# Large fp32r matmuls that read and write their columns as two halves in turn

## The chip, the cores and the metric

The kernel runs on one core of one Trainium2 chip. The metric is the device time of one execution in microseconds (us). One execution was profiled; its trace is what the prediction reads.

## What is computed

A trunk of two layers on x (1, 256, 2048) in float32. Each layer has a token mixer and a gated ConvFFN, and each of these is followed by `x <- LayerNorm(ALPHA * x + sublayer(x))`. Cut to what matters:

```python
def hgrn2_mixer(x, w_in, norm_g, w_out, lb):        # layer 0, w_in: (2048, 8192)
    q, f, i, g = split(x @ w_in)                     # gated recurrence over 16 heads
    ...
    return o @ w_out                                 # (2048, 2048)

def chunked_gmlp(x, w_in, ln_g, ln_b, w_s, b_s, w_out):   # layer 1, w_in: (2048, 4096)
    u, v = split(gelu(x @ w_in))
    ...
    return (u * gate) @ w_out

def conv_ffn(x, w_up, conv_w, conv_b, w_down):       # both layers, w_up: (2048, 11264)
    a, b = split(x @ w_up)
    a = causal_depthwise_conv(a, conv_w) + conv_b    # width 3
    return (silu(a) * b) @ w_down                    # (5632, 2048)
```

Nearly all of the arithmetic is in these products of 256 tokens with large weights.

## The kernel before

**Precision.** Every large product is made of three fp32r products. A float32 operand is split into a high part (its fp32r rounding) and a low part (what is left): `X` and `Y` hold the activations transposed, as `[128 partitions, 16 blocks of k, 2 parts, 256 tokens]`, high part first. A weight chunk (`fetch`, 1 MB by a DMA of the SP queue into `raw`) is split by `convert` into `hi` (a copy on ACT, line 93) and `lo` (a subtraction on DVE, line 94), each `[128, 4, 512]`. Chunks are planned in order (`want`), fetched and converted up to three ahead (`AHEAD`), in three buffers of each kind.

**block_a** has tokens on the output's partitions. The weights are the moving operand, 512 columns of 4 bytes; 128 tokens of an activation block are the stationary one. For each k-block there are three matmuls into one PSUM bank: high activations on high weights (line 123), high on low weights (line 124), low on high weights (line 125). It is used with `X` (a quarter of HGRN's input product, half of gMLP's) and with `Y` (all products on the way out). `staggered_pass` (lines 673 to 675) is the same loop, for the last chunk of HGRN's output product.

**block_b** has features on the output's partitions. A 128 x 128 block of the weights is stationary; the activations are the moving operand. `both` (line 159) streams the high and the low part of one k-block as 512 columns against the high weights, into the two halves of a bank; `rest` (line 166) streams the 256 high columns against the low weights into the bank's second half. They alternate, and `gather` adds the two halves when the block is done. In the first block of each FFN (`halves`), `both` is issued for 128 tokens at a time: 256 columns, two runs of 128.

TensorE issues in program order; in front of each matmul stands the load of its 128 x 128 stationary operand.

**Places.** `cp` holds a pad, `X`, a pad of `PAD_Y` bytes, `Y`, `z` and a pad of `PAD1`; `wp` holds three buffers each of `raw`, `hi` and, after a gap of `PAD_LO` bytes, `lo`. By these pads, in each partition, `X` and `hi` begin on a multiple of 256 bytes, `Y` and `lo` 128 bytes past one. A k-block takes 2048 bytes in `X` and `Y` (1024 for each part) and in `hi` and `lo`.

Of the kernel before, what the change touches and what calls it, by code (L numbers as in the profile page):

```python
# [15 lines left out]
P = 128  # L16
S = 256
# [9 lines left out]
CK = 4  # L27
# [2 lines left out]
FFN_GROUPS = (3, 4, 4)  # L30
AHEAD = 3
LINE = 256
PAD_Y = 128
PAD_LO = 128
PAD1 = 224
BLOCK = {1: 32, 4: 32, 16: 64}
XSEQ = ((0, 2, 4), (2, 2, 0), (4, 4, 1), (8, 4, 1), (12, 4, 0))
TURN_ACT = 3


class Trunk:
# [4 lines left out]
    def __init__(self, ctx, tc, a):  # L46
        self.tc = tc
        self.nc = nc = tc.nc
        self.a = a
        self.ctx = ctx  # L50
        ent = ctx.enter_context
        self.cp = ent(tc.tile_pool(name="cp", bufs=1))
        self.wp = ent(tc.tile_pool(name="wp", bufs=3))
        self.acc = ent(tc.tile_pool(name="acc", bufs=6, space=PSUM))
        self.misc = ent(tc.tile_pool(name="misc", bufs=2, space=PSUM))
        cp = self.cp
        cp.tile([P, LINE - 128], mybir.dt.uint8, name="pad0")
        self.X = cp.tile([P, NK, 2, S], F32R, name="X")
        cp.tile([P, PAD_Y], mybir.dt.uint8, name="pady")
        self.Y = cp.tile([P, NK, 2, S], F32R, name="Y")  # L60
        self.z = cp.tile([P, 2, D], F32, name="z")
        cp.tile([P, PAD1], mybir.dt.uint8, name="pad1")
        self.small = ent(tc.tile_pool(name="small", bufs=2))
        self.plan = []
        self.issued = 0
        self.taken = 0
        self.ready = []
# [15 lines left out]
    def convert(self, raw, extra, pieces=2):  # L83
# [3 lines left out]
        if not extra:  # L87
            pool.tile([P, PAD_LO], mybir.dt.uint8, tag="gap", name="gap", bufs=1)
        lo = pool.tile([P, CK, NB], F32R, tag="lo", name="wlo")
# [20 lines left out]
    def block_a(self, act, ka, w, k0, nch, c0, evac, staggered=False, halves=False):  # L110

        nc = self.nc
        ps = [self.acc.tile([P, NB], F32, tag="acc", name="pa") for _ in range(2)]
        n = [0, 0]

        def part(ch, ci, t):
            hi, lo = ch
            for kk in range(CK):
                k = ka + ci * CK + kk
                xh = act[:, k, 0, t * P : (t + 1) * P]  # L120
                xl = act[:, k, 1, t * P : (t + 1) * P]
                last = n[t] == nch * CK - 1
                nc.tensor.matmul(ps[t], xh, hi[:, kk, :], start=n[t] == 0, stop=False)  # L123
                nc.tensor.matmul(ps[t], xh, lo[:, kk, :], start=False, stop=False)  # L124
                nc.tensor.matmul(ps[t], xl, hi[:, kk, :], start=False, stop=last)  # L125
                n[t] += 1

        take = lambda ci: self.chunk(w, k0 + ci * CK, c0)
        first = max(0, nch - 4) if staggered else nch
        head = []  # L130
        if halves:
            head = [take(ci) for ci in range(min(3, nch))]
            for t in range(2):
                for ci, ch in enumerate(head):
                    part(ch, ci, t)
        for ci in range(len(head), first):
            ch = take(ci)
            for t in range(2):
                part(ch, ci, t)
        held = [take(ci) for ci in range(first, nch)]  # L140
        for t in range(2):
            for i, ch in enumerate(held):
                part(ch, first + i, t)
            if held:
                evac(t, ps[t])
        if not held:
            for t in range(2):
                evac(t, ps[t])

    def block_b(self, act, w, nch, c0, evac, halves=False):  # L150


        nc = self.nc
        ps = [self.acc.tile([P, 2, S], F32, tag="acc", name="pb") for _ in range(4)]
        last = nch * CK - 1

        def both(ch, k, j, s=slice(0, S), start=True):
            c = slice(j * P, (j + 1) * P)
            nc.tensor.matmul(  # L159
                ps[j][:, :, s], ch[0][:, k % CK, c], act[:, k, :, s],  # L160
                start=start and k == 0, stop=k == last, skip_group_check=halves,
            )

        def rest(ch, k, j):
            c = slice(j * P, (j + 1) * P)
            nc.tensor.matmul(  # L166
                ps[j][:, 1, :], ch[1][:, k % CK, c], act[:, k, 0, :],
                start=False, stop=False, skip_group_check=halves,
            )

        def one(ch, k, j):
            for m in (rest, both) if k else (both, rest):
                m(ch, k, j)

        first = 0
        if halves:
            first = nch
            held = [self.chunk(w, ci * CK, c0) for ci in range(nch)]
            for t in range(2):
                for k in range(last):  # L180
                    for j in range(4):
                        both(held[k // CK], k, j, slice(t * P, (t + 1) * P), t == 0)
            for k in range(last):
                for j in range(4):
                    rest(held[k // CK], k, j)
            for j in range(4):
                one(held[-1], last, j)
        for ci in range(first, nch):
            ch = self.chunk(w, ci * CK, c0)
            ks = range(ci * CK, (ci + 1) * CK)  # L190
            if ci < nch - 1:
                order = [(k, j) for k in ks for j in range(4)]
            else:
                order = [(k, j) for j in range(4) for k in ks]
            for k, j in order:
                one(ch, k, j)
        for j in range(4):
            evac(j, ps[j])
# [100 lines left out]
    def turn(self, t, k0, n=4, g=None, b=None):  # L299
# [7 lines left out]
        if g is not None:  # L307
            src = self.lnp.tile([P, n, P], F32, tag="turn", name="turn", bufs=2)
            for j in range(n):
                gk, bk = self.c(g, k0 + j), self.c(b, k0 + j)  # L310
                if j < TURN_ACT:
                    nc.scalar.activation(src[:, j, :], ps[:, j, :], AF.Identity, bias=bk, scale=gk)
# [348 lines left out]
    def staggered_pass(self, act, ka, w, k0):  # L661

        nc = self.nc
        ev = [self.add_z(c, last=True) for c in range(4)]
        held = [self.chunk(w, k0, c * NB) for c in range(4)]
        for t in range(2):
            for c in range(4):
                hi, lo = held[c]
                ps = self.acc.tile([P, NB], F32, tag="acc", name="pa")
                for kk in range(CK):  # L670
                    xh = act[:, ka + kk, 0, t * P : (t + 1) * P]
                    xl = act[:, ka + kk, 1, t * P : (t + 1) * P]
                    nc.tensor.matmul(ps, xh, hi[:, kk, :], start=kk == 0, stop=False)  # L673
                    nc.tensor.matmul(ps, xh, lo[:, kk, :], start=False, stop=False)  # L674
                    nc.tensor.matmul(ps, xl, hi[:, kk, :], start=False, stop=kk == CK - 1)  # L675
                ev[c](t, ps)


# [219 lines left out]
```

## Time and profile before

| | before |
|---|---|
| median of 3 runs | 2282.81 us (2282.72 to 2283.09) |
| the profiled execution | 2282.26 us |
| its span | 2280.6 us |
| granted TensorE clock | 0.998 |
| instructions of TensorE | 12781 matmuls, 12781 weight loads |
| HBM | 425.98 MB read, 188 GB/s over the span |

How to read the lines that follow. PE is TensorE's matmuls, PEld its weight loads, DVE the vector engine, ACT the scalar engine, POOL GpSimd, SP the engine whose queue issues the large DMAs. A group line has the line of the kernel, the engine, the operation, output and inputs by their names, shapes and count, then busy time in us and the mean of one in ns, then the idle time ahead of them. A line of a stretch has its two ends, its length, the busy time and the number of matmuls in it, the granted clock, the share of the DMA engines and GB/s. A piece of the chain has its start and its length in us, the engine, the tile, the line and how many instructions were merged. A line of the timeline has start and length in us. A matmul's length in the trace reaches past the start of the next one, so the distance of starts, and not the length, says how fast they follow each other.

### The profile page before, as it was taken

Reading aid. Unit: us, or ns where it says so; the run is one execution under the profiler, and the core shown is the slowest. Engines: PE = TensorE matmul, PEld = TensorE weight load, DVE = VectorE, ACT = ScalarE, POOL = GpSimd, SP = SyncE. Lnnn points to the kernel's source line nnn. Section 1 sums busy time; section 2 is a strip of 40 time slices with the busy share of each in tenths; the row PEclk is TensorE's granted clock in tenths of the full one; section 3 lists DMA queues with packets and bytes.
Section 4 is the critical chain, followed back from the end, with each engine's and each line's share of the span. In section 5 each row is a group of like instructions: output and inputs, shape, how many; then the busy total and the mean of one; then the engine's idle time right before and its main releaser. Section 6 shows DMA issues by size and latency. Waiting matters only on the chain.

```text
span 2280.6 us, 31751 instructions
## 1 busy us (share of the span) xinstructions
PE 2258.8 (99%) x12781; PEld 1925.7 (84%) x12781; DVE 1473.4 (65%) x2327; ACT 1105.4 (48%) x1698; POOL 48.5 (2%) x102
## 2 busy tenths in 40 slices
PE   8999999999999999999999999999999999999998
PEld 7888888889888888888888888888888888888886
DVE  5777677667665665456666676566765666465655
ACT  5666565545443444344444545455444444344542
POOL 3000000000000000000000000000000000000000
PEclk9999999999999999999999999999999999999999
DMA  7454645645565555555555676655565555555563
GB/s 260 151 181 140 198 149 167 206 166 200 186 227 196 186 185 187 199 186 185 187 196 175 208 218 183 230 177 181 185 234 180 196 186 193 193 185 187 183 203 111
DMA packets 214052, 430.14 MB, mean 189 GB/s; under 512 B 7544, under 2 KB 8336, under 8 KB 213904
## 3 DMA queue, kind: packets, MB, share of 16 engines
q1 hardware_dynamic: 209536, 415.26, 54.5%
q0 software_dynamic: 4368, 12.85, 1.9%
q8 instruction: 100, 1.64, 0.3%
q14 instruction: 48, 0.39, 0.0%
HBM read 425.98 MB, written 2.10 MB: 188 GB/s over the span
## 4 chain that ended last, share of the span: by engine, by line
PE 97%; DVE 2%; ACT 1%; DMA 0%; issue 0%; SPq 0%; DVEq 0%; ACTq 0%
PE pb L159 38%; PE pb L166 20%; PE pa L123 12%; PE pa L125 12%; PE pa L124 12%; DVE wlo L94 1%; PE pl L550 1%; PE pt L305 1%; ACT whi L93 0%; PE pg L752 0%; PE pa L673 0%; PE pa L675 0%; PE pa L674 0%; DMA z<-in_x_dram 0%; PE po L522 0%; PE pout L642 0%
## 5 line engine op out<-in xcount | busy, mean ns | idle before, releaser
L94 DVE TENSOR_TENSOR wlo<-raw,whi 128x1024 fp32r<-128x1024 f32 (+1 forms) x786 | 930.6, 1219 | 693.3 <-ACT whi L93 684.9
L159 PE MATMUL pb<-X,whi 128*128 128x512 f32 (+1 forms) x3960 | 1335.1, 388 | 1.9 <-DVE X L317 1.9
L93 ACT CAST whi<-raw 128x1024 fp32r<-128x1024 f32 (+1 forms) x786 | 790.2, 1047 | 894.8 <-PE pb L159 418.7
L166 PE MATMUL pb<-X,wlo 128*128 128x256 f32 x3840 | 1049.7, 281 | 0.0
L159 PEld LDWEIGHTS pb<-X,whi 128*128 128x128 f32 x3960 | 725.0, 188 | 160.1 <-DVE X L317 2.3
L166 PEld LDWEIGHTS pb<-X,wlo 128*128 128x128 f32 x3840 | 715.7, 189 | 6.1
L123 PE MATMUL pa<-whi,Y 128*128 128x512 f32 x928 | 365.4, 394 | 0.0
L125 PE MATMUL pa<-whi,Y 128*128 128x512 f32 x928 | 363.5, 392 | 0.0
L124 PE MATMUL pa<-wlo,Y 128*128 128x512 f32 x928 | 361.2, 389 | 0.0
L125 PEld LDWEIGHTS pa<-whi,Y 128*128 128x128 f32 x928 | 173.9, 187 | 40.4
L124 PEld LDWEIGHTS pa<-wlo,Y 128*128 128x128 f32 x928 | 174.3, 188 | 37.8
L123 PEld LDWEIGHTS pa<-whi,Y 128*128 128x128 f32 x928 | 174.9, 188 | 35.6
L204 ACT COPY rest<-pb 128x256 f32<-128x256 f32 x240 | 87.9, 369 | 110.9 <-PE pb L159 92.9
L123 PE MATMUL pa<-whi,X 128*128 128x512 f32 x256 | 101.8, 398 | 0.0
L124 PE MATMUL pa<-wlo,X 128*128 128x512 f32 x256 | 101.4, 396 | 0.0
L125 PE MATMUL pa<-whi,X 128*128 128x512 f32 x256 | 100.6, 393 | 0.0
L803 DVE SCALAR_TENSOR_TENSOR act<-a,cols,act 128x254 f32<-128x254 f32 (+1 forms) x176 | 73.2, 481 | 0.0
L125 PEld LDWEIGHTS pa<-whi,X 128*128 128x128 f32 x256 | 48.1, 188 | 11.8
L123 PEld LDWEIGHTS pa<-whi,X 128*128 128x128 f32 x256 | 48.1, 188 | 11.4
L124 PEld LDWEIGHTS pa<-wlo,X 128*128 128x128 f32 x256 | 48.2, 188 | 10.6
L397 DVE TENSOR_TENSOR z<-z,pa 128x512 f32<-128x512 f32 x40 | 27.4, 684 | 34.5 <-PE pa L125 30.3
L807 ACT ACTIVATE act<-act 128x256 f32<-128x256 f32 x88 | 33.8, 415 | 8.7 <-DVE act L803 8.5
(164 smaller groups left out, 1033.2 us busy)
## 6 DMA issues: line engine op xcount, KB each, us to landing
raw<-in_ffn_w_up_dram SPq DMA_DIRECT2D x176, 1024.0 KB, 4.9
raw<-in_ffn_w_down_dram SPq DMA_DIRECT2D x88, 1024.0 KB, 4.9
raw<-in_hg_w_in_dram SPq DMA_DIRECT2D x63, 1024.0 KB, 5.1
raw<-in_sg_w_in_dram SPq DMA_DIRECT2D x32, 1024.0 KB, 5.5
raw<-in_hg_w_out_dram SPq DMA_DIRECT2D x16, 1024.0 KB, 4.9
raw<-in_sg_w_out_dram SPq DMA_DIRECT2D x16, 1024.0 KB, 4.9
g<-in_ln_g_dram POOLq DMA_DIRECT2D x16, 256.0 KB, 6.5
b<-in_ln_b_dram POOLq DMA_DIRECT2D x16, 256.0 KB, 8.8
```

The costliest lines, as they stand in the source:

```text
L93: nc.scalar.copy(hi[:, s, :], raw[:, s, :])
L94: self.last_lo = nc.vector.tensor_tensor(lo[:, s, :], raw[:, s, :], hi[:, s, :].bitcast(F32), ALU.subtract)
L123: nc.tensor.matmul(ps[t], xh, hi[:, kk, :], start=n[t] == 0, stop=False)
L124: nc.tensor.matmul(ps[t], xh, lo[:, kk, :], start=False, stop=False)
L125: nc.tensor.matmul(ps[t], xl, hi[:, kk, :], start=False, stop=last)
L159: nc.tensor.matmul(ps[j][:, :, s], ch[0][:, k % CK, c], act[:, k, :, s], start=start and k == 0, stop=k == last, skip_group_check=halves,)
L166: nc.tensor.matmul(ps[j][:, 1, :], ch[1][:, k % CK, c], act[:, k, 0, :], start=False, stop=False, skip_group_check=halves,)
L204: nc.scalar.copy(r, ps[:, 1, :])
L305: nc.tensor.transpose(ps[:, j, :], self.z[:, t, k * P : (k + 1) * P], self.ident)
L397: nc.vector.tensor_tensor(zz, zz, ps, ALU.add)
L803: nc.vector.scalar_tensor_tensor(cv[:, d:], x[:, : S - d], self.c(("cw", l, 2 - d), f), cv[:, d:], ALU.mult, ALU.add,)
L807: nc.scalar.activation(cv, cv, AF.Silu)
```

## The change

Every large matmul of 512 columns, and `rest` with 256, gets its moving operand and its output through a new view `lines`: the columns are cut into two halves, and runs of `RUN` = 16 columns are taken from the first and the second half in turn. Each column still goes to its own place; only the order within a matmul is another. The halved matmuls of `both` keep theirs. The pad between `X` and `Y` is dropped, so that `Y` begins on a multiple of 256 bytes, as `X` and `hi` do; `PAD1` shrinks by 128, which leaves `hi` on such a multiple; the gap ahead of `lo` becomes 64 bytes.

```diff
-PAD_Y = 128
-PAD_LO = 128
-PAD1 = 224
+RUN = 16
+PAD_LO = 64
+PAD1 = 96
...
+def lines(x):
+
+    return x.rearrange("p (h n c) -> p n h c", h=2, c=RUN)
...
         self.X = cp.tile([P, NK, 2, S], F32R, name="X")
-        cp.tile([P, PAD_Y], mybir.dt.uint8, name="pady")
         self.Y = cp.tile([P, NK, 2, S], F32R, name="Y")
...
-                nc.tensor.matmul(ps[t], xh, hi[:, kk, :], start=n[t] == 0, stop=False)
-                nc.tensor.matmul(ps[t], xh, lo[:, kk, :], start=False, stop=False)
-                nc.tensor.matmul(ps[t], xl, hi[:, kk, :], start=False, stop=last)
+                o, h, l = lines(ps[t]), lines(hi[:, kk, :]), lines(lo[:, kk, :])
+                nc.tensor.matmul(o, xh, h, start=n[t] == 0, stop=False)
+                nc.tensor.matmul(o, xh, l, start=False, stop=False)
+                nc.tensor.matmul(o, xl, h, start=False, stop=last)
...
         def both(ch, k, j, s=slice(0, S), start=True):
             c = slice(j * P, (j + 1) * P)
+            o, x = ps[j][:, :, s], act[:, k, :, s]
+            if s.stop - s.start == S:
+                o, x = (lines(y.rearrange("p i t -> p (i t)")) for y in (o, x))
             nc.tensor.matmul(
-                ps[j][:, :, s], ch[0][:, k % CK, c], act[:, k, :, s],
+                o, ch[0][:, k % CK, c], x,
...
-                ps[j][:, 1, :], ch[1][:, k % CK, c], act[:, k, 0, :],
+                lines(ps[j][:, 1, :]), ch[1][:, k % CK, c], lines(act[:, k, 0, :]),
```

`staggered_pass` has the same edit as `block_a`.

More of the change, by code (lines that the diff above doesn't have):

```diff
@@ L672, in staggered_pass @@
                     xl = act[:, ka + kk, 1, t * P : (t + 1) * P]
-                    nc.tensor.matmul(ps, xh, hi[:, kk, :], start=kk == 0, stop=False)
-                    nc.tensor.matmul(ps, xh, lo[:, kk, :], start=False, stop=False)
-                    nc.tensor.matmul(ps, xl, hi[:, kk, :], start=False, stop=kk == CK - 1)
+                    o, h, l = lines(ps), lines(hi[:, kk, :]), lines(lo[:, kk, :])
+                    nc.tensor.matmul(o, xh, h, start=kk == 0, stop=False)
+                    nc.tensor.matmul(o, xh, l, start=False, stop=False)
+                    nc.tensor.matmul(o, xl, h, start=False, stop=kk == CK - 1)
                 ev[c](t, ps)
```

## The prediction

> **What bounds the kernel now.** I read the page's parts 1, 2 and 4 first, then the groups by shape, then the waits of TensorE, then stretches and chain pieces that hold one kind of matmul only.
>
> ```profile
> span 2280.6 us, 31751 instructions
> ...
> PE 2258.8 (99%) x12781; PEld 1925.7 (84%) x12781; DVE 1473.4 (65%) x2327; ACT 1105.4 (48%) x1698; POOL 48.5 (2%) x102
> ...
> HBM read 425.98 MB, written 2.10 MB: 188 GB/s over the span
> ...
> PE 97%; DVE 2%; ACT 1%; DMA 0%; issue 0%; SPq 0%; DVEq 0%; ACTq 0%
> ...
> raw<-in_ffn_w_up_dram SPq DMA_DIRECT2D x176, 1024.0 KB, 4.9
> ```
> ```profile
> PE pt L305 <- DMA z<-in_x_dram: 8.0, 2, 4.3
> PE pb L159 <- DVE X L317: 1.9, 2, 1.1
> ```
>
> TensorE is the chain: 97% of the path is PE, and its two longest waits sum to 9.9 us of 2280.6. So only the spacing of matmuls can move the end. A matmul's busy time is no spacing, because each one's record overlaps the next; the counts come from the groups by shape, the spacings from stretches.
>
> ```profile
> L159 PE MATMUL pb<-X,whi 128*128 128x512 f32 x3720 | 1304.6, 395 | 0.0
> L166 PE MATMUL pb<-X,wlo 128*128 128x256 f32 x3840 | 1049.7, 281 | 0.0
> L123 PE MATMUL pa<-whi,Y 128*128 128x512 f32 x928 | 365.4, 394 | 0.0
> ...
> L123 PE MATMUL pa<-whi,X 128*128 128x512 f32 x256 | 101.8, 398 | 0.0
> ...
> L159 PE MATMUL pb<-X,whi 128*128 128x256 f32 x240 | 30.8, 285 | 1.9 <-DVE X L317 1.9
> ...
> L673 PE MATMUL pa<-whi,Y 128*128 128x512 f32 x32 | 12.8, 399 | 0.0
> ```
> ```profile
> 720.00:890.00 170.00, 170.00 (x973) 1.00 0.57 186
> 900.00:980.00 80.00, 80.00 (x351) 1.00 0.58 195
> 1270.00:1320.00 50.00, 50.00 (x216) 1.00 0.64 211
> ```
> ```profile
> 513.06 5.03 PE pb L159 x42
> ...
> 530.43 7.23 PE pb L166 x61
> ...
> 1543.33 6.67 PE pb L159 x56
> 1549.99 7.23 PE pb L166 x61
> ```
> ```profile
> 1321.40 0.87 PE pw L718 x8
> ```
>
> The first fence gives counts (L124 and L125 stand as often as L123, L674 and L675 as often as L673): 512-column matmuls 3720 + 3 x 928 + 3 x 256 + 3 x 32 = 7368, the 256-column L166 3840, and 240 halves of L159. The second gives time, matmuls and granted clock (1.00, full) in stretches of one kind (block_b; block_a on Y; block_a on X); one or two of each count began before the stretch, which sets the spread. Spacings: a pair of block_b (L159 of 512 columns and L166 of 256) 2 x 170.00/972 = 349.8 ns; block_a on Y 80.00/349.5 = 228.9 ns (228.6 to 229.2); block_a on X 50.00/214.5 = 233.1 ns (232.6 to 233.6). The third has 256-column matmuls by themselves: halves of L159 (5.03 + 6.67)/98 = 119.4 ns, L166 14.46/122 = 118.5 ns. The fourth has 128-column matmuls, each with its own load of 128 weights: 0.87/8 = 109 ns. Together the groups that the change touches hold 3720 x 0.3498 + 120 x 0.1185 + 2880 x 0.2289 + 768 x 0.2331 = 2154 us, 94% of the span.
>
> **What is lost in a spacing.** The fp32r matmuls read two things at once: the moving operand, and the weights of the next matmul.
>
> ```profile
> 640.27 0.39 PE L159 MATMUL pb<-X,whi 128*128 128x512 f32 x1
> 640.28 0.19 PEld L166 LDWEIGHTS pb<-X,wlo 128*128 128x128 f32 x1
> 640.50 0.28 PE L166 MATMUL pb<-X,wlo 128*128 128x256 f32 x1
> 640.51 0.19 PEld L159 LDWEIGHTS pb<-X,whi 128*128 128x128 f32 x1
> 640.62 0.40 PE L159 MATMUL pb<-X,whi 128*128 128x512 f32 x1
> ```
>
> The next load starts with the matmul. It reads 512 bytes of a partition in about 109 ns, while the moving operand passes about 256 columns, 1024 bytes: twice the pace. That this is felt shows in block_a: on X and on Y the same instructions run on the same moving operand, and only the stationary one lies elsewhere (X, like the high weights, begins on a multiple of 256 bytes; Y, like the low ones, 128 past it). X costs 4.2 ns more. So the place of the two reads against each other, modulo some power of two, has a price.
>
> **The change, part by part.**
> (1) Order of columns. No matmul, load, wait or transfer is added or removed. Each 512-column matmul reads 16 columns (64 bytes) of one half, then 16 of the other 1024 bytes on (L166: 512 bytes on), and writes in the same order. Seen modulo 256 bytes, two runs lie on one place, so the moving operand now advances at 64 bytes per 32 columns, the pace of the load. Before, it lapped the load about twice in each load; now their distance stays what it is at the start. If that distance is clear, the loss goes.
> (2) Pads. Y moves 128 bytes down (a multiple of 256 again), the low weights stand 64 instead of 128 past the high ones. The distances are then 0 (activations against high weights) and 64 either way (against low ones). By itself a pad costs no instruction.
> (3) Evacuation reads the same PSUM places after the last matmul: nothing moves. The 240 halved matmuls (L159 with a slice) keep their order.
>
> What a spacing is without loss has no row, so I bound it. Upper end: a 512-column matmul less a 256-column one of the same line is 256 columns streamed while hardly any load is left: (349.8 - 118.5) - 119.4 = 111.9 ns. Lower end: the 109 ns of one load, below which an L166 cannot go, taken for each 256 columns. Since a load's record lasts 0.19 us and so reaches into the second half, 111.9 still holds some loss; I take the middle, 110.5 ns per 256 columns, 221 per 512.
> - block_b pairs: 349.8 - 331.5 = 18.3 ns x 3720 = 68.1 us
> - L166 alone: (118.5 - 110.5) x 120 = 1.0 us
> - Y: (228.9 - 221) x 2880 = 22.8 us (staggered_pass's 96 within)
> - X: (233.1 - 221) x 768 = 9.3 us
>
> Sum 101.2 us. With 111.9 it is 52.5 + 0.8 + 14.7 + 7.1 = 75; with 109 it is 84.8 + 1.1 + 31.4 + 11.6 = 129. Below zero the sum can go too: see the rivals. The profiled execution took 2282.26 us (span 2280.6), 0.55 below the median of 2282.81, so no correction: 2282.3 - 101.2 = 2181 us; 2207 and 2153 are the ends.
> The Trainium skill, "TensorE: Matmul & The Clock Gate", section "Back-to-back issue gap", gives N/2.4 + 2.5 ns, 215.8 and 109.2: as an estimate by that, the sum is 144 us and the time 2138.
>
> **What is late next.** A chunk of weights feeds 16 pairs, 5.6 us now, 5.3 then. Its transfer lands in 4.9 us with three chunks in flight, and the mean rate goes from 188 to 197 GB/s, under the 211 that a stretch above already moves. Its conversion is cover enough too:
>
> ```profile
> L94 DVE TENSOR_TENSOR wlo<-raw,whi 128x1024 fp32r<-128x1024 f32 (+1 forms) x786 | 930.6, 1219 | 693.3 <-ACT whi L93 684.9
> ...
> L93 ACT CAST whi<-raw 128x1024 fp32r<-128x1024 f32 (+1 forms) x786 | 790.2, 1047 | 894.8 <-PE pb L159 418.7
> ```
>
> 2 x 1.05 us on ACT, then 2 x 1.22 on DVE per chunk; DVE's share goes from 65% to 68%. So nothing of the gain should come back as a wait.
>
> **The rivals.**
> *Jumps cost* (the other side). A matmul of 512 columns now has 32 runs, 31 jumps on both the read and the write side; L166 has 15: 7368 x 31 + 3840 x 15 = 286,008 jumps. The only jump now in the trace is the one in each half of L159 (two runs of 128 columns): 119.4 against 118.5 ns for the L166 that has none, 0.9 ns if all of it is the jump's. Then the loss is 257 us against 101 won: 2282.3 + 156 = 2438 us. It decides from 101.2 us/286,008 = 0.35 ns a jump upward. Against it: L166 loads other weights than L159 does, so the 0.9 is no clean price, and may be zero. The Trainium skill, "PSUM — Partial Sum Buffer", section "Specifications (TRN2)", speaks for this rival: its lines of PSUM are 8 bytes and any access that isn't contiguous is said to slow matmuls much. No row here shows that for runs of 64 bytes.
> *Meeting throughout.* With equal pace a bad starting distance lasts for the whole load. Now a lap spends roughly half its way near the load (64 bytes each way of 256); a meeting that never ends would double the loss: +101, 2383 us. Were it only the distance 0 (3840 L166, 2432 of block_a), their loss (52 us) and the other matmuls' gain (49) would about cancel: 2285. For it: the loads start with the matmul in the rows above, and distance 0 stands for more than half of the matmuls. Against it: the loss on X's distance 0 differs from Y's 128 by only 4.2 ns.
> *No effect.* The loss belongs to each matmul and not to meetings: 2282 us. The Trainium skill, the TensorE page again, section "Step-by-step: what each phase is for", says that the two reads have ports of their own and a load takes nothing from the running matmul. The 4.2 ns between X and Y, in the stretches above, disagree.
>
> **How the numbers follow.** Forecast 0.68; no effect 0.10; jumps cost 0.12; meeting throughout 0.10. A measurement tells 0.2%, 4.6 us, from no change. Faster: 0.68 and 0.02 of no effect (pads alone) = 0.70. Same: 0.07 of it and 0.01 of jumps near 0.35 ns = 0.08. Slower: 0.01 + 0.11 + 0.10 = 0.22. The forecast's own range is 2138 (all loss gone, and more than the rows promise) to 2265 (a sixth of the gain). To hold 8 in 10 it takes in no effect and the jumps up to about 0.5 ns, (0.5 - 0.35) x 286,008 = 42 us above 2282: 2138 to 2325, which leaves out 0.09 of meeting throughout, 0.07 of jumps and 0.03 below.
>
> **What will show it.** In block_b's stretches a pair at about 331 ns (now 349.8); block_a at about 221 on both X and Y, so that their difference is gone: that is the step of the equal pace. The 128-column and halved matmuls stay at 109 and 119.4. If the 512-column matmuls lengthen and L166 by half as much, jumps cost; if only matmuls at one distance lengthen (L123 against L124), it is the meeting. TensorE's waits should stay near 10 us. The forecast is wrong if a jump costs a third of a nanosecond, or if the starting distance of the two reads, which no row shows, is a bad one.

## The result: slower, and the profile after

The changed kernel takes 2355.65 us (median of 4 runs, 2355.60 to 2355.93) against 2282.85 beside it: a ratio of 1.0319, 95% interval 1.0301 to 1.0337. The forecast was 2181, the range 2138 to 2325; it is 73 us slower, on the other side and out of the range.

The page of the changed kernel, and the longest waits of its TensorE:

```profile
span 2353.9 us, 31751 instructions
...
PE 2333.6 (99%) x12781; PEld 1948.8 (83%) x12781; DVE 1474.2 (63%) x2327; ACT 1104.7 (47%) x1698; POOL 48.3 (2%) x102
...
PE 98%; DVE 1%; DMA 0%; issue 0%; ACT 0%; SPq 0%; DVEq 0%
```
```profile
PE pt L313 <- DMA z<-in_x_dram: 7.8, 2, 4.1
PE pb L167 <- DVE X L325: 1.8, 2, 1.1
```

DVE and ACT do the same work in the same time, TensorE waits for no more than before, and the chain is TensorE. So the 73 us lie in the spacing of matmuls. The stretches of one kind (block_b, block_a on Y, block_a on X; the columns as before: ends, length, busy time and matmuls, granted clock, DMA share, GB/s), and then pieces of the chain:

```profile
740.00:910.00 170.00, 170.00 (x946) 1.00 0.55 184
930.00:1010.00 80.00, 80.00 (x335) 1.00 0.55 184
1308.00:1358.00 50.00, 50.00 (x210) 1.00 0.64 210
```
```profile
543.18 7.32 PE pb L174 x61
...
1591.04 6.68 PE pb L167 x56
```
```profile
1361.61 0.88 PE pw L727 x8
```

A pair of block_b went from 349.8 to 359.8 ns (2 x 170.00/945), block_a on Y from 228.9 to 239.9 (80.00/333.5), on X from 233.1 to 239.8 (50.00/208.5). L166, now L174, by itself takes 120.0 (7.32/61) for 118.5. The kinds that were not edited stay: 56 halves in 6.68 us for 6.67, 128-column matmuls 110 ns for 109. Summed: 10.0 x 3720 + 11.0 x 2880 + 6.7 x 768 = 74 us, the whole loss. And the difference between X and Y is gone, but upwards: every 512-column matmul now takes about 240. That the two became equal is no sign of the equal pace; the pads alone do it, as the second experiment shows.

### The profile page after: what moved, and what is told of

Same layout as the page of the kernel before. It is cut to its first block, busy times and chain, and to the rows that moved or that the text cites. A ratio compares the mean times of both kernels' runs of the same rounds, so it can differ in the third digit from the quotient of the medians.

```text
span 2353.9 us, 31751 instructions
## 1 busy us (share of the span) xinstructions
PE 2333.6 (99%) x12781; PEld 1948.8 (83%) x12781; DVE 1474.2 (63%) x2327; ACT 1104.7 (47%) x1698; POOL 48.3 (2%) x102
## 4 chain that ended last, share of the span: by engine, by line
PE 98%; DVE 1%; DMA 0%; issue 0%; ACT 0%; SPq 0%; DVEq 0%
PE pb L167 39%; PE pb L174 20%; PE pa L129 12%; PE pa L128 12%; PE pa L130 12%; PE pl L558 1%; PE pt L313 1%; DVE wlo L98 0%; PE pa L683 0%; PE pa L682 0%; PE pa L684 0%; PE pg L761 0%; DMA z<-in_x_dram 0%; PE pout L650 0%; PE pl L626 0%; PE po L530 0%
## 5 line engine op out<-in xcount | busy, mean ns | idle before, releaser
L167 PE MATMUL pb<-X,whi 128*128 128x512 f32 (+1 forms) x3960 | 1373.5, 396 | 1.8 <-DVE X L325 1.8
L174 PE MATMUL pb<-X,wlo 128*128 128x256 f32 x3840 | 1064.8, 285 | 0.0
L167 PEld LDWEIGHTS pb<-X,whi 128*128 128x128 f32 x3960 | 739.7, 192 | 182.3 <-DVE X L325 2.3
L174 PEld LDWEIGHTS pb<-X,wlo 128*128 128x128 f32 x3840 | 715.3, 189 | 7.2
L129 PE MATMUL pa<-wlo,Y 128*128 128x512 f32 x928 | 375.3, 404 | 0.0
L128 PE MATMUL pa<-whi,Y 128*128 128x512 f32 x928 | 373.9, 403 | 0.0
L130 PE MATMUL pa<-whi,Y 128*128 128x512 f32 x928 | 372.9, 402 | 0.0
L403 DVE SCALAR_TENSOR_TENSOR z<-z,pa 128x512 f32<-128x512 f32 x32 | 21.9, 685 | 27.9 <-PE pa L130 27.9
```

Of the source, the lines that this page charges most:

```text
L128: nc.tensor.matmul(o, xh, h, start=n[t] == 0, stop=False)
L129: nc.tensor.matmul(o, xh, l, start=False, stop=False)
L130: nc.tensor.matmul(o, xl, h, start=False, stop=last)
L167: nc.tensor.matmul(o, ch[0][:, k % CK, c], x, start=start and k == 0, stop=k == last, skip_group_check=halves,)
L174: nc.tensor.matmul(lines(ps[j][:, 1, :]), ch[1][:, k % CK, c], lines(act[:, k, 0, :]), start=False, stop=False, skip_group_check=halves,)
```

## The experiments

Theories in the order in which they came. R: the cost is on the reading side of the changed order; W: on the writing side; M: the moving operand and the next weights meet throughout; J: every jump costs the same; L: every stretch of 64 bytes that is read costs a clock, and another where the next one isn't its neighbour; P: every run of the access pattern has a fixed price; T: the loss belongs to the length of a turn; B: the two halves hit one another because of their distance. Their times are in the expectations.

### One side at a time

```diff
-                o, h, l = lines(ps[t]), lines(hi[:, kk, :]), lines(lo[:, kk, :])
+                o, h, l = plain(ps[t]), lines(hi[:, kk, :]), lines(lo[:, kk, :])    # read_turns
+                o, h, l = lines(ps[t]), plain(hi[:, kk, :]), plain(lo[:, kk, :])    # write_turns
```

(`plain` keeps the columns in order; block_b and staggered_pass likewise.)

> The moving operand is read in turns of 16 columns as in the changed kernel, the output is written contiguously (so columns land in permuted order: the products are not the reference's). Same pads as the changed kernel. Theory R (a jump costs on the reading side): as the changed kernel, 512-column matmuls about 239 ns apart, L166's kind about 121, near 2355 us. Theory W (a jump costs on the writing side of PSUM): the cost goes; with equal pace the 512-column matmuls come to 214 to 222 ns, below 2220 us. Theory M (the two reads meet throughout, jumps are free): as the changed kernel, since the reads are the same, near 2355 us.

> The output is written in turns of 16 columns, the moving operand is read contiguously (permuted order again). Pads of the changed kernel. Theory R: no reading jumps, so near the kernel before with other pads, 512-column matmuls 226 to 236 ns, 2240 to 2310 us. Theory W: the jumps stay, 239 ns or more, 2355 us or more, since the reads meet as before on top. Theory M: the reads lap each other as before, so near the kernel before, about 2283 us.

Turns of the read alone: 2355.61 us, the changed kernel to within 0.1. Turns of the write alone: 2281.85, beside 2281.91 for the kernel before. The same stretches, of read_turns and then of write_turns:

```profile
740.00:910.00 170.00, 170.00 (x946) 1.00 0.54 184
930.00:1010.00 80.00, 80.00 (x335) 1.00 0.53 184
```
```profile
720.00:890.00 170.00, 170.00 (x981) 1.00 0.55 189
900.00:980.00 80.00, 80.00 (x346) 1.00 0.58 197
```

Read in turns, 946 and 335 matmuls fit into the stretches, exactly the changed kernel's counts; written in turns, 981 and 346. That these are not the counts of the kernel before (973 and 351) is the work of the pads, which the next run has by themselves. Theory W falls: 31 jumps a matmul in PSUM cost nothing that shows. The Trainium skill, "PSUM — Partial Sum Buffer", section "Specifications (TRN2)", has any access that isn't contiguous slow matmuls much; for runs of 64 bytes this run, 2281.85 us, disagrees.

### The pads alone

```diff
-PAD_LO = 128
-PAD1 = 224
+PAD_LO = 64
+PAD1 = 96
-        cp.tile([P, PAD_Y], mybir.dt.uint8, name="pady")
```

> The order of columns of the kernel before with the pads of the changed one: what the pads do by themselves. Theories R and W: the changed kernel's loss is the jumps', so this is near the kernel before, within 30 us of 2283 either way, with classes of matmuls that differ by a few ns as before. Theory M: the pads alone change little here too, since contiguous reads lap; the same range. If this alone is near 2355, all three fall and the pads are the cause.

2282.78 us beside 2281.91: no difference in the total. Its stretches (block_b, block_a on Y, on X):

```profile
720.00:890.00 170.00, 170.00 (x981) 1.00 0.56 190
900.00:980.00 80.00, 80.00 (x346) 1.00 0.59 197
1270.00:1320.00 50.00, 50.00 (x217) 1.00 0.66 212
```

The total hides two moves in opposite directions. A pair of block_b went from 349.8 to 346.9 ns (2 x 170.00/980), some 11 us less over 3720 pairs; block_a on Y from 228.9 to 232.2 (80.00/344.5), some 10 us more over 2880 matmuls; on X from 233.1 to 232.0 (50.00/215.5). With X and Y on the same place modulo 256 bytes, contiguous matmuls on the two are equal as well. Against these pads the turns of the read cost 12.9 ns a pair and 7.7 to 7.8 ns a matmul of block_a.

And the turns with the pads of the kernel before:

```diff
-PAD_LO = 64
-PAD1 = 96
+PAD_LO = 128
+PAD_Y = 128
+PAD1 = 224
+        cp.tile([P, PAD_Y], mybir.dt.uint8, name="pady")
```

> The turns of 16 of the changed kernel with the pads of the kernel before: the distances are then 0 (X on high weights, Y on low ones) and 128 (X on low weights, Y on high ones) in place of 0 and 64. Theory R: 239 to 241 ns for every 512-column class, 2355 us. Theory M: classes at distance 128 come down to 214 to 222 ns (L159's kind in block_b, two of three in block_a on Y), those at 0 stay near 239: 2260 to 2300 us.

2362.91 us. At distance 128, where M wanted 214 to 222 ns, no class of 512-column matmuls came under 238 (block_a on Y 242.2 on average). M falls in the kernel; R stands. That it is 7 us more than with the new pads was not foreseen: the classes on Y rose to 240 to 243 and one on X to 246. So in the kernel the place still moves a spacing that is read in turns.

### Turns of 32 columns

```diff
-RUN = 16
+RUN = 32
```

> Turns of 32 columns in place of 16: 15 jumps for 31 in a 512-column matmul, 7 for 15 in a 256-column one. Theories R and W (cost by the jump, 0.8 ns each from 239.4 less 512 columns without any loss): 512-column matmuls 12 to 13 ns closer than in the changed kernel, about 226, L166's about 6 closer, about 115, unless the reads meet again: 2240 to 2270 us. Theory M: the pace modulo 256 bytes is the same over 64 columns, so the meeting stays, near 2355 us.

2319.61 us, outside both: about half of the loss (37.7 of 73 us) at about half the jumps, with a pair of block_b in 353 ns and a matmul on Y in 237. I took this for a constant price of a jump, (2355.6 - 2282.3) us/286,008 = 0.256 ns (theory J), and asked the next runs for it.

### Bursts of one kind

Behind the last product of the kernel before, bursts of equal matmuls on X whose results nobody reads. Only the read is in turns there; the output is written in order:

```diff
+        w = flat[:, 4096 + at // 4 : 4096 + at // 4 + weights]
+        for _ in range(17):
+            nc.tensor.matmul(o, w, x, start=True, stop=True)
```

> The kernel before, and behind its last product 33 bursts of 17 matmuls each on X, whose results nobody reads: contiguous and in turns, with the next weights 0 to 224 bytes past the moving operand modulo 256, with 128 or only 32 columns of weights to load (32 leave three quarters of the load out), turns of 8 to 128 columns, and halves 1024, 1088, 1152, 1280 or 2048 bytes apart. Theory R (each jump of the read costs by itself): turns of 16 take about 239 ns at every distance and with 32 columns of weights as well; turns of 8 some 12 to 26 ns more, turns of 32, 64 and 128 come down to the contiguous one by the number of jumps. Theory M (the cost is the meeting of the two reads at equal pace): some distance in the sweep is clear, near 128 bytes, with 214 to 222 ns, and with 32 columns of weights the turns of 16 lose most of their excess, 216 to 222 ns, as the contiguous ones do, whatever the length of a turn. The whole kernel takes about 2283 + 33 x 17 x 0.23 less what the tail hides, 2400 to 2415 us.

The timeline of TensorE at the end of that run (start, length, line, operation, shapes, count). The spacing is the distance of two bursts' starts over 17 matmuls each; `plain` is contiguous, `turns` are of 16 columns, the number is the place of the weights in bytes past the moving operand modulo 256, `few` has 32 columns of weights, `short` is 256 columns:

```profile
2269.51 4.03 PE L848 MATMUL plain0at<-X 128*128 128x512 f32 x17
2273.38 4.12 PE L848 MATMUL plain32at<-X 128*128 128x512 f32 x17
...
2293.21 4.07 PE L848 MATMUL plain192at<-X 128*128 128x512 f32 x17
2297.12 4.13 PE L848 MATMUL plain224at<-X 128*128 128x512 f32 x17
2301.09 4.24 PE L848 MATMUL turns0at<-X 128*128 128x512 f32 x17
...
2333.72 4.10 PE L848 MATMUL plain_few<-X 128*32 128x512 f32 x17
2337.66 20.25 PE L848 MATMUL turns_few<-X 128*32 128x512 f32 x85
...
2390.38 2.20 PE L848 MATMUL short_turns<-X 128*128 128x256 f32 x17
2392.42 2.20 PE L848 MATMUL short_turns_few<-X 128*32 128x256 f32 x17
```

Turns of 16 take (2333.72 - 2301.09)/136 = 239.9 ns over all eight places, each of them 240.0 once the first matmuls are past, and the 256-column ones 2.04/17 = 120.0. That is 7.5 ns for each turn, whatever the place. With a quarter of the load the turns of 16 take the same 240.0 (the second 17 of turns_few). Contiguous matmuls spread with the place: 227.6 at 0, 230.0 at 192, 233 at most others. But with a quarter of the load, at place 0, they take 3.94/17 = 231.8, more than the 227.6 with the whole load there: less load does not make them faster at that place. So M falls for the turns; for contiguous reads the place counts, and the amount of load, where it was varied, doesn't. J is in doubt too: within turns_few, 512 columns in turns of 8 took 243 ns, of 32 about 235, and of 64 and 128 231.5 to 231.8, no more than contiguous (these from the single starts, since the line merges five bursts). Turns of 64 and 128 have the same form of access pattern as turns of 16, so the form by itself isn't the cost.

### What length of turn, and does its place matter

A second set of bursts (`past`: the moving operand begins 0, 16, 32 bytes past a multiple of 256), with a sweep of layouts of which more below:

```diff
+    for at in (0, 4, 8):
+        burst(f"turns{4 * at}past", turned(16, 256, at), 512)
...
+    for a in range(0, 512, 64):
+        for b in range(0, 512, 64):
...
+                    nc.tensor.matmul(o[:, 1, :], Y[:, lo + c : lo + c + P], k.X[:, kk, 0, :], start=True, stop=True)
+                    nc.tensor.matmul(o, Y[:, hi + c : hi + c + P], k.X[:, kk, :, :], start=True, stop=True)
```

> The kernel before, and behind its last product more bursts whose results nobody reads. First 25 of 17 matmuls with 32 columns of weights: contiguous ones of 128 to 512 columns, ones that begin 16, 32 or 48 bytes past a multiple of 256, turns of 16 that begin there, turns of 8 to 80 columns (of halves of 240 columns, or of 256 where the turn doesn't divide 240), and the same 16, 32 or 64 columns read again and again. Then 64 layouts of weights against activations (high weights 0 to 448 bytes past them modulo 512, low ones likewise), each with 32 matmuls in block_b's order and 24 in block_a's. Theory L (a lost clock of 0.42 ns for each 64-byte line that is read, and another where the next line isn't its neighbour: 17 x 0.417 = 7.08 ns for 16 columns in a row, 7.5 ns in turns, as 240.0 for 32 turns says): contiguous 7.08 ns per 16 columns plus up to 5 ns, so 113 for 256 and 213 for 480; turns of 16 that begin 32 bytes past a line touch two lines each and take about 253; the same 16 columns again take 227 to 240. Theory P (a fixed price of each run of the access pattern, whatever the lines): turns that begin 32 bytes past stay at 240, the same 16 columns again take 240, and contiguous spacing is not tied to 16 columns. The layouts: by either theory the contiguous matmuls spread from 227 to 235 ns by place, block_b's pairs from 340 to 352, and the layout of the kernel before need not be the best one.

```profile
2270.01 2.17 PE L845 MATMUL plain256cols<-X 128*32 128x256 f32 x17
2272.02 2.61 PE L845 MATMUL plain320cols<-X 128*32 128x320 f32 x17
...
2292.46 4.03 PE L845 MATMUL plain32past<-X 128*32 128x512 f32 x17
2296.32 4.10 PE L845 MATMUL plain48past<-X 128*32 128x512 f32 x17
...
2300.26 4.24 PE L845 MATMUL turns0past<-X 128*32 128x512 f32 x17
2304.34 4.25 PE L845 MATMUL turns16past<-X 128*32 128x512 f32 x17
2308.43 4.24 PE L845 MATMUL turns32past<-X 128*32 128x512 f32 x17
2312.51 4.02 PE L845 MATMUL turns8of<-X 128*32 128x480 f32 x17
```

The turns take 4.08 to 4.09 us each: 240 ns also where every turn of 64 bytes lies across a multiple of 64. Theory L, which wanted 253 there, is out. The same 16 columns read again and again took 235 on average, in an uneven 219 to 245, which is not the even 240 of P; the turns of 12 below rule P's fixed price out. Contiguous, with a quarter of the load, 256 columns take 2.01/17 = 118.2 ns, and 512 columns that begin 32 bytes later take 3.86/17 = 227.1. A third set, with halves of 240 columns:

```diff
+    for run in (4, 6, 8, 10, 12, 16, 20, 24, 30, 40, 60, 120):
+        burst(f"few{run}run", run)
+    for run in (0, 12, 16, 24, 48):
+        for at in (0, 64, 128, 192):
+            burst(f"all{run}run{at}at", run, 128, at=at)
```

> The kernel before and more bursts, 33 matmuls of 480 columns each, unread: turns of 4 to 120 columns with 32 columns of weights; contiguous and turns of 12, 16, 24 and 48 with all 128 columns of weights, which begin 0, 64, 128 or 192 bytes past the moving operand modulo 256; and turns of 16 and of 12 with the halves 1040 to 4096 bytes apart. Theory T: the spacing follows the length of the turn and not the number of jumps: turns of 12 and 24 near 216 ns, 16 and 8 near 227, 20 near 224, with all weights as with few, and turns of 16 stay at 225 to 229 however far the halves are apart. Theory B (the two halves hit one another because they are a multiple of 256 bytes apart): turns of 16 come down to about 216 at some other distance of the halves, turns of 12 are fast at all. Theory M, if anything is left of it: with all weights turns of 12 or 24 differ by place by more than 3 ns.

Turns of 4 to 30 columns with 32 columns of weights, 33 matmuls of 480 columns in each burst (the halves 1024 bytes apart), then all weights, contiguous (`all0run`) and in turns of 12, 16 and 24, four places each:

```profile
2270.83 7.86 PE L846 MATMUL few4run<-X 128*32 128x480 f32 x33
2278.53 9.84 PE L846 MATMUL few6run<-X 128*32 128x480 f32 x33
2288.20 7.65 PE L846 MATMUL few8run<-X 128*32 128x480 f32 x33
2295.69 8.99 PE L846 MATMUL few10run<-X 128*32 128x480 f32 x33
2304.52 7.28 PE L846 MATMUL few12run<-X 128*32 128x480 f32 x33
2311.63 7.63 PE L846 MATMUL few16run<-X 128*32 128x480 f32 x33
2319.10 7.53 PE L846 MATMUL few20run<-X 128*32 128x480 f32 x33
2326.47 7.31 PE L846 MATMUL few24run<-X 128*32 128x480 f32 x33
2333.62 7.97 PE L846 MATMUL few30run<-X 128*32 128x480 f32 x33
2341.43 7.32 PE L846 MATMUL few40run<-X 128*32 128x480 f32 x33
```
```profile
2362.93 7.32 PE L846 MATMUL all0run0at<-X 128*128 128x480 f32 x33
...
2391.60 7.33 PE L846 MATMUL all12run0at<-X 128*128 128x480 f32 x33
...
2420.38 7.64 PE L846 MATMUL all16run0at<-X 128*128 128x480 f32 x33
...
2450.29 7.41 PE L846 MATMUL all24run0at<-X 128*128 128x480 f32 x33
...
2479.05 7.35 PE L846 MATMUL all48run0at<-X 128*128 128x480 f32 x33
```

By the distance of starts over 33: turns of 4 take 233 ns, of 6 293, of 8 227, of 10 268, of 12 215, of 16 226, of 20 223, of 24 217, of 30 237. With all weights, over four places (132 matmuls): contiguous 28.67/132 = 217.2, turns of 12 218.0, of 16 226.6, of 24 217.9. So 40 turns of 12 columns cost nothing against contiguous reads, and 30 turns of 16 cost 9.4 ns. The number of jumps doesn't decide; at this distance of the halves the length does, as T has it. Lengths that are no multiple of 4 columns (6, 10, 30) are worst. B falls: with the halves 1040, 1056, 1088, 1152, 1216, 2048 or 4096 bytes apart, turns of 16 took 226.5 to 226.9 every time. (In the first set one burst of 512 columns, with the halves 1152 bytes apart, took 242; the others 240.) Turns of 12, fast at 1024, 2048 and 4096, took 221 to 230 at the other distances, which T did not foresee: their spacing depends on where the halves lie, and in this set that of the 16s doesn't.

### Back in the kernel: turns of 64 and of 8

```diff
-RUN = 16
+RUN = 64    # run64
+RUN = 8     # run8
```

> The changed kernel with turns of 64 columns: 7 jumps in a 512-column matmul, 3 in a 256-column one, 63,096 in all. Theory J (each jump costs the same, 73.3 us for 286,008, so 0.256 ns): 16 us over the kernel before, near 2298 us. Theory T (the loss belongs to particular lengths of a turn, as the bursts have it: 16 columns 240.0 ns, 64 columns 231.4 against 231.6 contiguous): no loss, 2278 to 2286 us.

> The changed kernel with turns of 8 columns: 63 jumps in a 512-column matmul, 31 in a 256-column one, 583,224 in all. Theory J: 149 us over the kernel before, near 2431 us. Theory T (bursts: 242.9 ns against 240.0 for turns of 16): 3 ns for each of 7368 and 1.5 for each of 3840 over the changed kernel, 2375 to 2390 us.

2281.28 us and 2387.89 us, beside 2282.24. Both are where T and the bursts put them; J is 17 and 43 us off. The stretches of run64 hold 981, 347 and 217 matmuls, those of the pads alone within one. So J, which fitted run32 by its total, is refuted.

### Another layout, contiguous

The sweep in the second set of bursts gave pairs in block_b's order for high weights (rows) and low weights (columns) so many bytes past X modulo 256, in ns:

```
          lo 0     64    128    192
hi   0   353.3  346.9  346.7  346.7
    64   349.9  352.3  349.9  353.2
   128   351.9  347.2  350.4  347.4
   192   341.0  347.2  347.4  348.9
```

With 256 bytes more on either side the entries repeat within 1.3 ns, but for two: the first (346.8 to 346.9 elsewhere), and low 256 with high 64 or 320 (353.1 for 349.9). First and last start of L871 in the layout of the kernel before (0, 128) and in the best one (192, 0):

```profile
2380.34 0.28 PE L871 MATMUL hi0lo128b<-X,Y 128*128 128x256 f32 x1
...
2385.53 0.28 PE L871 MATMUL hi0lo128b<-X,Y 128*128 128x256 f32 x1
```
```profile
2625.18 0.28 PE L871 MATMUL hi192lo0b<-X,Y 128*128 128x256 f32 x1
...
2630.29 0.28 PE L871 MATMUL hi192lo0b<-X,Y 128*128 128x256 f32 x1
```

Fifteen pairs in 5.19 and in 5.11 us (the table takes the starts unrounded). In the kernel before, contiguous, that layout is two pads:

```diff
-PAD_Y = 128
-PAD_LO = 128
+PAD_Y = 64
+PAD_LO = 64
```

> The kernel before, contiguous, with other pads: high weights 192 bytes past X modulo 256 and low ones 0, Y 64. In the sweep of layouts that pair took 341.6 ns in block_b against 346.7 for the layout of the kernel before, 234.1 against 233.5 in block_a on X, and 230.8 against 230.0 on Y. If the place of weights against activations is what spreads the contiguous matmuls, 5.1 x 3720 - 0.6 x 768 - 0.8 x 2880 = 16 us less than the kernel before, 2262 to 2272 us. If the spread of the sweep doesn't carry over to the kernel (its pairs took 349.8 there, not 346.7): within 5 us of 2283.

2262.17 us (median of 4, 2261.57 to 2262.78) against 2282.24: a ratio of 0.991, interval 0.9894 to 0.9927. That is 0.9% less than the kernel before, and the interval leaves out 1. Its stretches (block_b, block_a on Y, on X):

```profile
712.00:882.00 170.00, 170.00 (x997) 1.00 0.57 193
890.00:970.00 80.00, 80.00 (x348) 1.00 0.57 189
1255.00:1305.00 50.00, 50.00 (x215) 1.00 0.61 198
```

997 matmuls of block_b in 170 us, where 973 went before: a pair in 341.4 ns (2 x 170.00/996) for 349.8, by this 31 us over 3720 pairs. Block_a gives a little back (230.9 on Y for 228.9, 6 us; 234.2 on X for 233.1, 1 us). By the stretches that is 24 us, for 20 measured. The sweep promised 16 us and the kernel gave 20, since its pairs had stood at 349.8 and not at the sweep's 346.7. For this layout (341.0 in the sweep, 341.4 in the kernel) and for that of the pads alone (346.9 in both) sweep and kernel agree; why they don't for the layout before stays open.

## Why the prediction was wrong

**What bounds the kernel.** Right: only the spacing of matmuls moved the end, and nothing behind TensorE became late.

**What is lost in a spacing.** This step failed. It read the 4.2 ns between X and Y as a price of meeting the next load, which was right in so far as place does matter (the sweep spreads over 12 ns a pair, and the pads alone bring X and Y together at 232). But it put the whole distance from 231 to 221 ns down to meetings. With a quarter of the load, contiguous matmuls still take 231.8 ns, and the bursts at their best place come to 227, not to 221. The 221 was mis-sized from the start: 111.9 ns is what 256 further columns add to a matmul that already runs, and it was taken as the upper end for a whole matmul of 256. By themselves 256 columns take 118.2 ns with a quarter of the load, as L166 did with all of it (118.5). What the excess over 221 consists of is not shown; no contiguous burst of 512 columns came under 227. The 215.8 and 109.2 ns behind the lower end of the range were not reached either: the contiguous bursts took 227 or more, and 118.

**Order of columns, part (1).** The sum took the new order to stream as fast as an undisturbed old one. It takes 7.5 ns in the bursts for each turn of 16 columns, 240 and 120 ns for 512 and 256; the contiguous read takes 227 to 234 for 512. Equal pace was to take the place out of the spacing. In the bursts it did, 240.0 ns at all eight places, above all the spacings that place gives a contiguous read there; in the kernel with the old pads the classes still spread from 238 to 246. The forecast gain of 68.1 + 22.8 + 9.3 us became losses of 37, 32 and 5.

**Pads, part (2).** No instruction, as said, and nothing in the total. That the total stood still was luck: some 11 us won in block_b and 10 lost in block_a on Y. **Evacuation, part (3).** Nothing, as said. **What is late next.** Nothing, but never put to the test.

**The rivals.** *Jumps cost* had the side, and the reading half of its mechanism. Its price didn't hold: 0.9 ns from one jump of a 128-column run gave 2438, and the cost isn't by the jump at all. Turns of 64 in the kernel, and of 64 and 128 in the bursts, cost nothing, so the 0.9 was no price of a jump. The break-even of 0.35 ns was drawn from a gain that didn't exist; at 0.256 ns a jump the change already lost 73 us. *Meeting throughout* gave 2383, nearest the measured time, by a mechanism that three runs refute. *No effect* came nearest in its reading of the kernel before, since less load did not shorten the spacing of 512 columns. The Trainium skill, "TensorE: Matmul & The Clock Gate", section "Step-by-step: what each phase is for", was cited for it: a load takes nothing from the running matmul. The 231.8 ns with a quarter of the load, no less than with all of it, agree; the sweep, 341 to 353 ns a pair by the place of the weights alone, does not.

What could have warned: the halved matmuls were taken as a witness for jumps although their runs are 128 columns, eight times the new ones. Nothing in the trace read 16 columns at a time, and the range should have reached further up for that.

**Open.** Why turns of 16 take 7.5 ns each in the bursts, at every place, either load and, but for one burst, every distance of the halves, while turns of 12 and 24 can be free. What makes a contiguous read of 512 columns take 227 ns or more. And why weights 192 and 0 bytes past the activations are the best of the sweep. The runs show these as facts; they don't show the mechanism.

## What to carry to other kernels

When TensorE is the chain, count matmuls in stretches of one kind and watch the spacing: that carries this whole result. Do it for each kind, since the pads alone moved two kinds in opposite directions under a total that stood still. Before an order of reads is rewritten, measure the order by itself in a burst behind the kernel, since a form that the trace has never run has no price in it, and a total that fits one theory (half the jumps, half the loss) can belong to another. Where weights lie against activations modulo 256 bytes is worth a sweep: two pads gave 0.9%.

## What the runs showed of the hardware

- A moving fp32r operand read in turns of 16 columns streams at 7.5 ns a turn: 240.0 ns for 512 columns, 120.0 for 256, with 32 or 128 columns of weights to load and, for 512, at eight places of the weights. In the kernel, classes of 512 columns took 238 to 246 ns.
- Turns whose length is no multiple of 16 bytes cost more than all others tried: 480 columns took 293 ns in turns of 6, 268 in turns of 10 and 237 in turns of 30, against 215 to 233 in turns of 4 to 24 that are such a multiple, and 217 contiguous.
- Writing PSUM in runs of 16 columns cost nothing: 2281.85 us, for 2282.78 with the same pads and 2281.91 in the kernel before.
- The place of weights against activations modulo 256 bytes moved a pair of contiguous matmuls (512 and 256 columns) between 341 and 353 ns.
